# One group of experts fetched by rows from DRAM, and the last pair's output in column ranges

## The chip, the cores and the metric

The kernel runs on one core of a Trainium2 chip. Its time is the device time of one execution in microseconds (us), of which the median over several executions is given. The engines of the core are TensorE (PE, matrix products; PEld is its weight load), VectorE (DVE), ScalarE (ACT), GpSimd (POOL) and SyncE (SP). SP does no arithmetic here: it issues nearly all transfers. A name with q behind it (SPq) is an engine's instruction queue. A core has 16 DMA engines, and each transfer of this kernel is spread over them.

## The reference, cut to what matters

One decoder block on 512 tokens of width 1024, all in float32: a mixer (linear attention beside block-sparse attention), an attention into 256 memory tokens, and a layer of 32 experts, each with a residual add, and a last normalisation. The change lies in the expert layer and behind it.

```python
g_prob = softmax(xt @ w_rg + b_rg); p_grp, grp = top_k(g_prob, 1)      # one of 4 groups
top_p, top_i = top_k(softmax(e_in), 2)                                # two of its 8 experts
weights = p_grp * top_p / sum(top_p); expert = grp * 8 + top_i
# for each expert e with its tokens tok and their weights w:
xb = xt[tok]                                                          # rows of h, 1024 wide
yb = (silu(xb @ w_gate[e]) * (xb @ w_up[e])) @ w_down[e] * w[:, None] # inner width 512
out[tok] += yb
# behind all experts
return rmsnorm(x + out, g_final)
```

## The kernel before, in words

The first half of the kernel (mixer, memory attention, router) ends at about 486 us of the profiled execution. Behind it the 32 experts are worked through as 16 pairs (0 to 15), each expert with 64 slots for tokens; a token's code is its expert and its slot. What doesn't fit 64 slots is done in a loop (`overflow`) that runs as often as the router's result asks; it stands in pair 15, after its second step.

**Gather.** Two pairs, four experts, share one gather of 256 slots: `group_hots` (VectorE) makes 0/1 matrices `oh` (token by slot), and `gather` multiplies them on TensorE with the normalised rows. These are held as two tiles per 128 tokens, `xrh` and `xrl` (a rounded part and the rest, which together give the row). One of its eight steps gives 128 of the 1024 features for 256 slots: 8 products into `g_ps`, then a copy by ScalarE into `xT`, with the gain `gfeat`. The steps are laid between other work of the odd pair and of the even pair behind it. Pairs 0 and 1 have their own gather inside the router's code; seven gathers stand in the loop over the pairs, for pairs 2 and 3 (here called group 1), 4 and 5, and so on.

**One pair.** Eight steps `gate_up` (each two k-rows of gate and up weights for two experts, into `gu_ps`), `hidden` (Silu on ScalarE, a product on VectorE), four transposes `hidden_t`, four steps `down` into `y_ps`, a split into a rounded part and a rest (`rows_hilo`: yh on ScalarE, yl on VectorE), and `combine`: products of yh and yl with the 0/1 rows `ot` into `c_ps`, which VectorE adds into `x`. The `combine` of a pair stands among the steps of the next.

**Weights.** Each pair takes 24 loads of 512 KB (16 of gate and up, 8 of down), 384 in all; below they are numbered 1 to 384 in the order of issue. SP issues them in program order (`load_gate_up`, L938; `load_down`, L944). `eload(n)` lets them be written up to number n at a place of the program: about 33 ahead of the pair at work. Every load takes a block of the pool `bp` (48 blocks of 4 KB per partition); blocks are given out in program order, also to other tiles (`oh`, `xT`, `gf`), and a load waits until the former user of its block is done, and until the load eight before it on SP's queue has landed. `SPILL = 15, 2, 372` says where the loop stands and that loads up to 372 are written ahead of it; the other twelve stand behind it, and every engine passes through the loop's branch (L1267).

**The end.** In the last pair the left 512 columns of `y_ps` are made first, then the right ones; each half is multiplied, added into `x`, squared and summed (`sqj`), the left half is multiplied by the last gain on POOL (`xg`), and `finish` scales and stores: right halves from VectorE through SP's queue (L1389), left halves from ScalarE through its own (L1391).

The order on each engine is that in which the program writes the instructions down; nothing reorders them.

## Time and profile before

| what | value |
|---|---|
| median of 3 executions | 971.14 us (970.98 to 971.64) |
| the profiled execution | 969.94 us |
| its span, first to last instruction | 968.1 us |
| granted TensorE clock, mean | 0.997 |
| PE / DVE / ACT / POOL busy | 949.3 / 471.4 / 312.2 / 32.6 us |
| moved by DMA | 252.47 MB, 250.55 MB of it through one queue |
| DMA share of the span, by queue | 70.2% + 0.3% + 0.3% + 0.3% |

All times in the profile are of one execution. A group row names line, engine, operation and tiles; behind the bar stand its busy time and the mean duration in ns. A row of the chain of waits has a start, a length and what the time went to: an instruction of an engine, or a transfer for which it waited. A row of the windows has the busy time of each engine in that stretch with the number of instructions, the granted clock, and the share and rate of the DMA engines.

### The profile page before, as it was taken

The page shows a single profiled execution, that of the slowest core. Times are in us where ns is not written, and L with a number is a line of the kernel's source. Part 1 is how long each engine was busy: PE and PEld are TensorE (multiplying, and loading weights), DVE is VectorE, ACT ScalarE, POOL GpSimd, SP SyncE. Part 2 cuts the span into 40 slices and gives each one's busy share as a digit, 9 for nine tenths or more (in the row PEclk, how much of TensorE's full clock was granted, in tenths as well). Part 3 has the DMA queues.
Part 4 walks back from the last instruction along what each step waited for, and adds up shares of the span by engine and source line. Part 5 has one row for each costly group of instructions (what it writes and reads, how often), then busy time and mean ns, then how long its engine had stood idle before and what let it go on. Part 6 is the DMA issues. An engine that isn't in the chain of part 4 may idle for free.

```text
span 968.1 us, 13248 instructions
## 1 busy us (share of the span) xinstructions
PE 949.3 (98%) x4969; PEld 619.2 (64%) x4969; DVE 471.4 (49%) x1047; ACT 312.2 (32%) x639; POOL 32.6 (3%) x46
## 2 busy tenths in 40 slices
PE   9999999999999999999999999999999999999995
PEld 7888888878878888888835445454454543545432
DVE  5344872554557846466733254341544414344234
ACT  6452643545565424455321102111021110201103
POOL 3200010000000000000000000000000000000003
PEclk9999999999999999999999999999999999999998
DMA  9512347223253605482689999999999999999983
GB/s 296 171 44 64 68 68 194 65 66 88 66 196 131 196 1 153 124 336 92 260 339 409 408 409 409 409 409 410 408 410 409 409 408 408 409 408 409 409 317 147
DMA packets 114086, 252.47 MB, mean 261 GB/s; under 512 B 10310, under 2 KB 55651, under 8 KB 114020
## 3 DMA queue, kind: packets, MB, share of 16 engines
q1 hardware_dynamic: 113444, 250.55, 70.2%
q10 hardware_dynamic: 576, 1.05, 0.3%
q8 instruction: 40, 0.66, 0.3%
q14 instruction: 26, 0.21, 0.1%
HBM read 247.90 MB, written 3.67 MB: 260 GB/s over the span
## 4 chain that ended last, share of the span: by engine, by line
PE 92%; DVE 3%; ACT 3%; DMA 1%; issue 1%; ACTq 0%; SPq 0%; DVEq 0%
PE gu_ps L136 22%; PE y_ps L136 12%; PE fo L131 8%; PE fo L133 7%; PE fo L132 7%; PE g_ps L136 7%; PE c_ps L136 6%; PE ro L133 3%; PE ro L131 3%; PE ro L132 3%; PE x2o L136 2%; PE xo L132 1%; PE xo L133 1%; PE xo L131 1%; PE mo_ps L136 1%; PE s_ps L136 1%
## 5 line engine op out<-in xcount | busy, mean ns | idle before, releaser
L136 PE MATMUL gu_ps<-we,xT 128*64 128x512 f32 x1024 | 229.0, 595 | 0.4 <-ACT xT L1045 0.3
L136 PEld LDWEIGHTS gu_ps<-we,xT 128*64 128x64 f32 x1024 | 71.0, 137 | 134.0 <-issue 121.5
L206 DVE TENSOR_TENSOR wlo<-wraw,whi 128x1024 fp32r<-128x1024 f32 (+1 forms) x71 | 86.2, 1231 | 77.2 <-ACT whi L205 76.9
L136 PE MATMUL y_ps<-we,hid_t 128*64 128x512 f32 x512 | 114.2, 596 | 0.7 <-ACT hid_t L1238 0.7
L1230 DVE SCALAR_TENSOR_TENSOR hid<-hid,ws,gu_ps 128x512 f32<-128x512 f32 x16 | 12.0, 747 | 171.2 <-PE gu_ps L136 171.2
L131 PE MATMUL fo<-hTh,whi 128*128 128x512 f32 x224 | 89.1, 398 | 0.0
L132 PE MATMUL fo<-hTl,whi 128*128 128x512 f32 x224 | 87.5, 390 | 0.0
L133 PE MATMUL fo<-hTh,wlo 128*128 128x512 f32 x224 | 87.4, 390 | 0.0
L1263 DVE TENSOR_TENSOR x<-c_ps,x 128x512 f32<-128x512 f32 x120 | 75.0, 683 | 20.7 <-PE c_ps L136 20.7
L136 PEld LDWEIGHTS y_ps<-we,hid_t 128*64 128x64 f32 x512 | 35.9, 137 | 69.8 <-issue 60.0
L205 ACT ACTIVATE whi<-wraw 128x1024 fp32r<-128x1024 f32 (+2 forms) x73 | 74.8, 1045 | 4.2 <-DMA wraw<-in_w_in_dram 4.1
L136 PE MATMUL g_ps<-oh,xrh 128*128 128x256 f32 x256 | 66.0, 299 | 1.4 <-DVE oh L1028 1.4
L136 PEld LDWEIGHTS g_ps<-oh,xrh 128*128 128x128 f32 x256 | 47.0, 189 | 30.7 <-issue 24.3
L136 PE MATMUL g_ps<-oh,xrl 128*128 128x256 f32 x256 | 61.6, 281 | 0.0
L1229 ACT ACTIVATE hid<-gu_ps 128x512 f32<-128x512 f32 x16 | 9.6, 597 | 156.8 <-PE gu_ps L136 156.8
L205 ACT ACTIVATE yh<-y_ps 128x512 fp32r<-128x512 f32 x32 | 19.1, 598 | 115.1 <-PE y_ps L136 115.1
L1203 ACT ACTIVATE xT<-g_ps,gfeat 128x256 f32<-128x256 f32 x56 | 25.8, 474 | 89.2 <-PE g_ps L136 57.6
L136 PE MATMUL c_ps<-yh,ot 128*128 128x512 f32 x128 | 52.0, 406 | 0.7 <-ACT yh L205 0.7
L136 PE MATMUL c_ps<-yl,ot 128*128 128x512 f32 x128 | 50.6, 395 | 0.2 <-DVE yl L206 0.2
L131 PEld LDWEIGHTS fo<-hTh,whi 128*128 128x128 f32 x224 | 42.1, 188 | 10.1 <-issue 1.9
L133 PEld LDWEIGHTS fo<-hTh,wlo 128*128 128x128 f32 x224 | 42.0, 188 | 9.1
L136 PEld LDWEIGHTS g_ps<-oh,xrl 128*128 128x128 f32 x256 | 47.1, 189 | 0.6
(321 smaller groups left out, 1487.4 us busy)
## 6 DMA issues: line engine op xcount, KB each, us to landing
we<-in_w_exp_gate_dram SPq DMA_DIRECT2D x128, 512.0 KB, 10.2
we<-in_w_exp_up_dram SPq DMA_DIRECT2D x128, 512.0 KB, 10.2
we<-in_w_exp_down_dram SPq DMA_DIRECT2D x128, 512.0 KB, 10.2
wraw<-in_w_in_dram SPq DMA_DIRECT2D x38, 512.0 KB, 4.1
wraw<-in_w_out_dram SPq DMA_DIRECT2D x8, 512.0 KB, 5.5
wraw<-in_w_ckv_dram SPq DMA_DIRECT2D x8, 512.0 KB, 4.8
wraw<-in_w_proj_gla_dram SPq DMA_DIRECT2D x4, 512.0 KB, 4.3
wraw<-in_w_proj_moba_dram SPq DMA_DIRECT2D x4, 512.0 KB, 4.4
```

The costliest lines, as they stand in the source:

```text
L131: PE.matmul(o, lh, rh, start=first, stop=False)
L132: PE.matmul(o, lh, rl, start=False, stop=False)
L133: PE.matmul(o, ll, rh, start=False, stop=last)
L136: PE.matmul(o, l, r, start=first, stop=last, **kw)
L205: S.activation(hi, src, AF.Copy)
L206: eng.tensor_tensor(lo, src, f(hi), op=ALU.subtract)
L1203: S.activation(xT[k], o, AF.Copy, scale=gfeat[:, k:k + 1])
L1229: S.activation(row, gu[0][0:n], AF.Silu)
L1230: V.scalar_tensor_tensor(row, row, ws[:, 0:1], gu[1][0:n], op0=ALU.mult, op1=ALU.mult)
L1263: V.tensor_tensor(xs, o, xs, op=ALU.add)
```

## The change

Four things are changed.

1. **Group 1 is fetched.** At the end of the router POOL adds `xrh` and `xrl` to four tiles `xp` (blocks of the pool, taken ahead of the loads that are written after them), and stores them through its own queue as a table `xd` of 512 rows in DRAM. It also loads a row of token numbers, `tok`. In pairs 0 and 1, at step k = 5, `fetch` finds on VectorE the token of each of the 128 slots of pairs 2 and 3, and POOL issues an indirect transfer that takes the 128 rows from `xd` into a tile `rows`. `turn` then transposes it in eight squares on TensorE, and ScalarE copies them with the gain into `xT`. `group_hots` and `gather` of group 1 are gone. (The router's token for an empty slot is 0; its weight is 0.)
2. **The loop's limit** goes from 372 to 376 loads.
3. **The last pair's down weights** come as column halves: two blocks of 512 columns and 256 rows, per expert and half, instead of four blocks of whole rows.
4. **The last pair's output** is made in three column ranges, 0 to 511, 512 to 767 and 768 to 1023. The scaled row is written in place into `xo`; three tiles of 128 tokens are stored as whole rows through SP, the last one as two halves.

```diff
-    early = np.concatenate([tri, upper, onehot], axis=1)
+    tokens = np.tile(np.arange(T, dtype=np.float32), (P, 1))
+    early = np.concatenate([tri, upper, onehot, tokens], axis=1)
...
-    SY.dma_start(early, c_early)
+    SY.dma_start(early, c_early[:, 0:512])
...
+    def load_down_halves(e):
+
+        for c in range(2):
+            for q in range(2):
+                b = blk("we", [2, 512])
+                rows = w_exp_down[0][e][2 * q * P:(2 * q + 2) * P, 512 * c:512 * c + 512]
+                SY.dma_start(b, rows.rearrange("(k p) n -> p k n", p=P))
+                yield b
...
-            for loads, n in ((load_gate_up, 2), (load_down, 1)):
+            for loads, n in ((load_gate_up, 2), (load_down_halves if p == NE // 2 - 1 else load_down, 1)):
...
+    xd = dp.tile([T, D], F32, name="xd")
+    for t in range(NT):
+        xp = blk("xp", [D])
+        G.tensor_tensor(xp, f(xrh[t]), f(xrl[t]), op=ALU.add)
+        G.dma_start(xd[tcol(t), :], xp)
+    tok = med("tok", [T])
+    G.dma_start(tok, c_early[:, 512:])
...
+    def fetch(codes):
+
+        oa, ws, idx = med("oa", [T]), small("ws", [2]), small("idx", [1], I32)
+        for i in range(2):
+            V.scalar_tensor_tensor(oa, cw[0][:, i, :], codes, tok, op0=ALU.is_equal, op1=ALU.mult,
+                                   accum_out=ws[:, i:i + 1])
+        V.tensor_tensor(idx, ws[:, 0:1], ws[:, 1:2], op=ALU.add)
+        b = blk("rows", [D])
+        G.indirect_dma_start(b, None, xd[:, :], bass.IndirectOffsetOnAxis(ap=idx[:, 0:1], axis=0))
+        return b
+
+    def turn(rows, xT):
+
+        b = blk("xT", [KD, P])
+        xT.extend(b[:, k, :] for k in range(KD))
+        for k in range(0, KD, 2):
+            t_ps = ps("xt_ps", [2, P])
+            for j in range(2):
+                PE.transpose(t_ps[:, j, :], rows[:, tcol(k + j)], ident)
+            for j in range(2):
+                S.activation(xT[k + j], t_ps[:, j, :], AF.Copy, scale=gfeat[:, k + j:k + j + 1])
+            yield
...
-        s0 = (p % 2) * P
+        s0 = 0 if p // 2 in FETCH else (p % 2) * P
...
-            if p % 2 and p + 1 < NP and k == OH_AT:
+            if (p + 2) // 2 in FETCH and k == 5:
+                fetched[p + 2] = fetch(sid[:, 2 * p + 4:2 * p + 5])
+            if p % 2 and p + 1 < NP and k == OH_AT and (p + 1) // 2 not in FETCH:
                 oh_next = group_hots((p + 1) // 2)
-        if p % 2 and p + 1 < NP:
+        if (p + 1) // 2 in FETCH:
+            xT = []
+            gat = turn(fetched.pop(p + 1), xT)
+        elif p % 2 and p + 1 < NP:
             xT = []
             gat = gather(oh_next, xT, 4 * CAP)
...
-        gs = 1 if p % 2 and p + 1 < NP else 0
+        gs = 1 if (p % 2 or p // 2 in FETCH) and p + 1 < NP else 0
...
-    def last_products(c):
-
-        y = rows_hilo(y_ps[c])
-        yield
-        o = [ps("c_ps", [512]) for t in range(NT)]
+    ranges = (0, 512), (512, 256), (768, 256)
+    ssq, xo = [small("ss4", [4]) for t in range(NT)], [blk("xo", [D]) for t in range(NT)]
+    r = [small("rr", [1]) for t in range(NT)]
+    for t in range(NT):
+        V.memset(ssq[t][:, 3:4], EPS)
+    y_ps.append(ps("y_ps", [256]))
+
+    def x_part(i, t):
...
+    def y_part(i):
+        return y_ps[i][:, 0:ranges[i][1]]
+
+    def last_down(i, fts):
+        a, n = ranges[i]
+        c, a = divmod(a, 512)
+        for ft in fts:
+            for e, (b, own) in enumerate(zip(w, halves)):
+                mm(y_ps[i][own, 0:n], hid_t[:, ft, 64 * e:64 * e + 64], b[8 + 2 * c + ft // 2][:, ft % 2, a:a + n],
+                   ft == 0, ft == 3, skip_group_check=True)
...
+    y = [[med(q, [n], F32R) for q in ("yh", "yl")] for _, n in ranges]
+
+    def high(i):
+        S.activation(y[i][0], y_part(i), AF.Copy)
+
+    def low(i):
+        V.tensor_tensor(y[i][1], y_part(i), f(y[i][0]), op=ALU.subtract)
+
+    def products(i):
+        n = ranges[i][1]
+        o = [ps("c_ps", [512 // n, n]) for _ in range(NT * n // 512)]
...
         for t in range(NT):
-            product(o[t], ot, t, y)
-        yield
-        for t in range(NT):
-            xs = x_half(t, c)
-            V.tensor_tensor(xs, o[t], xs, op=ALU.add)
-            if c == 0 and t == NT - 1:
-                yield
-            S.activation(blk("sqj", [512]), xs, AF.Square, scale=1.0 / math.sqrt(D), accum_out=ssq[t][:, c:c + 1])
-            if c == 0:
-                xg[t] = blk("xg", [512])
-                G.tensor_tensor(xg[t], xs, gf[:, 0:512], op=ALU.mult)
+            product(o[t], ot, t, y[i])
+        return o
+
+    def add(o, i, t):
+        V.tensor_tensor(x_part(i, t), o[t], x_part(i, t), op=ALU.add)
+
+    def square(i, t):
+        S.activation(blk("sqj", [512])[:, 0:ranges[i][1]], x_part(i, t), AF.Square, scale=1.0 / math.sqrt(D),
+                     accum_out=ssq[t][:, i:i + 1])
+
+    def gains(t):
+        G.tensor_tensor(xo[t][:, 0:512], x_part(0, t), gf[:, 0:512], op=ALU.mult)
...
     def scale(t):
         ms = small("ms", [1])
-        V.scalar_tensor_tensor(ms, ssq[t][:, 0:1], EPS, ssq[t][:, 1:2], op0=ALU.add, op1=ALU.add)
...
-        G.tensor_tensor(r, ms, neghalf[:, 0:1], op=ALU.pow)
-        return r
-
-    def finish(t, r):
-        o = blk("xo", [512])
-        V.scalar_tensor_tensor(o, x_half(t, 1), r, gf[:, 512:1024], op0=ALU.mult, op1=ALU.mult)
-        SY.dma_start(out[tcol(t), 512:1024], o)
-        S.activation(xg[t], xg[t], AF.Copy, scale=r)
-        S.dma_start(out[tcol(t), 0:512], xg[t])
-
...
-    for t in range(NT + 1):
-        if t < NT:
-            r[t] = scale(t)
-        if t:
-            finish(t - 1, r[t - 1])
+        V.tensor_reduce(ms, ssq[t], axis=AX.X, op=ALU.add)
+        G.tensor_tensor(r[t], ms, neghalf[:, 0:1], op=ALU.pow)
+
+    def low_half(t):
+        S.activation(xo[t][:, 0:512], xo[t][:, 0:512], AF.Copy, scale=r[t])
+
+    def high_half(t):
+        V.scalar_tensor_tensor(xo[t][:, 512:], x_sb[t][:, 512:], r[t], gf[:, 512:], op0=ALU.mult, op1=ALU.mult)
+
+    last_down(0, range(4))
+    high(0)
+    low(0)
+    last_down(1, range(4))
+    high(1)
+    low(1)
+    last_down(2, range(2))
...
+    last_down(2, range(2, 4))
+    for t in range(NT):
+        add(o0, 0, t)
+        square(0, t)
+        gains(t)
+    for t in range(NT):
+        add(o1, 1, t)
+        if t == 1:
+            high(2)
+        square(1, t)
+        if t == 2:
+            low(2)
+    o2 = products(2)
+    for t in range(NT):
+        add(o2, 2, t)
+        square(2, t)
+        if t >= 2:
+            scale(t - 2)
+    for t in range(NT):
+        if t == 0:
+            scale(2)
+        low_half(t)
+        high_half(t)
+        if t == 0:
+            scale(3)
+        if t + 1 < NT:
+            SY.dma_start(out[tcol(t), :], xo[t])
+    S.dma_start(out[tcol(t), 0:512], xo[t][:, 0:512])
+    SY.dma_start(out[tcol(t), 512:], xo[t][:, 512:])
...
-SPILL = 15, 2, 372
+FETCH = (1,)
+SPILL = 15, 2, 376
```

PE at the end of pair 1's `gate_up` (`xT_3826` is the right half of the first gather's result; the numbers behind `xrh` and `xrl` count tiles of 128 tokens), before:

```order
L136 MATMUL gu_ps<-we,xT_3826 64x512 x16
L136 MATMUL g_ps<-oh,xrh_3812 128x256
L136 MATMUL g_ps<-oh,xrl_3816 128x256
L136 MATMUL g_ps<-oh,xrh_3813 128x256
L136 MATMUL g_ps<-oh,xrl_3817 128x256
L136 MATMUL g_ps<-oh,xrh_3814 128x256
L136 MATMUL g_ps<-oh,xrl_3818 128x256
L136 MATMUL g_ps<-oh,xrh_3815 128x256
L136 MATMUL g_ps<-oh,xrl_3819 128x256
L136 MATMUL c_ps<-yh,ot 128x512
L136 MATMUL c_ps<-yl,ot 128x512
```

and with the change:

```order
L137 MATMUL gu_ps<-we,xT_3826 64x512 x16
L1243 MATMUL xt_ps<-keep,rows 128x128 x2
L137 MATMUL c_ps<-yh,ot 128x512
L137 MATMUL c_ps<-yl,ot 128x512
L137 MATMUL c_ps<-yh,ot 128x512
L137 MATMUL c_ps<-yl,ot 128x512
L1278 MATMUL ht_ps<-keep,hid 128x128 x4
L1243 MATMUL xt_ps<-keep,rows 128x128 x2
```

Eight products of one gather step have become two transposes, which read the fetched tile `rows`; three more such places follow in pair 1, and four in pair 2 for pair 3.

POOL at the start of the experts, with the change (`rr` is the last of the router's normalisations; before, the read of the loop's count, L1306 there, stood right behind it):

```order
L918 TENSOR_TENSOR rr<-ms,neghalf 128x1 x4
L1161 TENSOR_TENSOR xp<-xrh_3812,xrl_3816 128x1024
L1162 DMA xd<-xp 128x1024
L1161 TENSOR_TENSOR xp<-xrh_3813,xrl_3817 128x1024
L1162 DMA xd<-xp 128x1024
L1161 TENSOR_TENSOR xp<-xrh_3814,xrl_3818 128x1024
L1162 DMA xd<-xp 128x1024
L1161 TENSOR_TENSOR xp<-xrh_3815,xrl_3819 128x1024
L1162 DMA xd<-xp 128x1024
L1164 DMA tok<-in_c_early_dram 128x512
L1233 DMA rows<-xd,idx 128x1024 x2
L1348 TENSOR_LOAD rt_xi
```

Ten instructions have come in, seven of them transfers, in this order on one queue.

SP's loads 35 to 40 with the change, with what each waits for (a name with DMAHW is a landing of one of SP's own transfers, DMASW one of POOL's, PE and Pool are the engines that used the block before):

```order
L939 DMA we_4737<-in_w_exp_gate_dram 128x1024 [waits DMAHW7_49,DMASW0_49,Pool_49]
L939 DMA we_4749<-in_w_exp_up_dram 128x1024 [waits DMAHW0_49,PE_49]
L939 DMA we_4751<-in_w_exp_gate_dram 128x1024 [waits DMAHW1_49,PE_49]
L939 DMA we_4753<-in_w_exp_up_dram 128x1024 [waits DMAHW2_49,DMASW1_49,Pool_49]
L939 DMA we_4755<-in_w_exp_gate_dram 128x1024 [waits DMAHW3_49,PE_49]
L939 DMA we_4771<-in_w_exp_up_dram 128x1024 [waits DMAHW4_49,DMASW2_49,Pool_49]
```

Before, each of these waited for its DMAHW and for PE alone. Now loads 35, 38 and 40 (and 45) wait for the landing of a copy into `xd`, whose tile `xp` had the block.

More of the change, by code (lines that the diff above doesn't have):

```diff
@@ L1299, in block_kernel @@
     slot, spill = None, spill_list()
-    comb, gat = iter(()), iter(())
+    comb, gat, fetched = iter(()), iter(()), {}
     for p in range(NP):
@@ L1353, in block_kernel @@
         comb = combine(ot, ys)
-    ssq, xg, r = [small("ss2", [2]) for t in range(NT)], {}, {}
-    def x_half(t, c):
-        return x_sb[t][:, 512 * c:512 * c + 512]
-    def last_products(c):
-        y = rows_hilo(y_ps[c])
-        yield
-        o = [ps("c_ps", [512]) for t in range(NT)]
-        for t in range(NT):
-            product(o[t], ot, t, y)
-        yield
-        for t in range(NT):
-            xs = x_half(t, c)
-            V.tensor_tensor(xs, o[t], xs, op=ALU.add)
-            if c == 0 and t == NT - 1:
-                yield
-            S.activation(blk("sqj", [512]), xs, AF.Square, scale=1.0 / math.sqrt(D), accum_out=ssq[t][:, c:c + 1])
-            if c == 0:
-                xg[t] = blk("xg", [512])
-                G.tensor_tensor(xg[t], xs, gf[:, 0:512], op=ALU.mult)
+    ranges = (0, 512), (512, 256), (768, 256)
@@ new lines, in block_kernel @@
+    y = [[med(q, [n], F32R) for q in ("yh", "yl")] for _, n in ranges]
[6 more added lines that the diff above has]
+        o = [ps("c_ps", [512 // n, n]) for _ in range(NT * n // 512)]
+        o = [b[:, q, :] for b in o for q in range(512 // n)]
+        for t in range(NT):
+            product(o[t], ot, t, y[i])
+        return o
@@ L1382, in scale @@
-        r = small("rr", [1])
-        G.tensor_tensor(r, ms, neghalf[:, 0:1], op=ALU.pow)
-        return r
-    def finish(t, r):
-        o = blk("xo", [512])
-        V.scalar_tensor_tensor(o, x_half(t, 1), r, gf[:, 512:1024], op0=ALU.mult, op1=ALU.mult)
-        SY.dma_start(out[tcol(t), 512:1024], o)
-        S.activation(xg[t], xg[t], AF.Copy, scale=r)
-        S.dma_start(out[tcol(t), 0:512], xg[t])
-    part = [last_products(c) for c in range(2)]
-    for ft in range(4):
-        down(y_ps, hid_t, ft, w, (0,))
@@ L1396, in block_kernel @@
-    next(part[0])
-    for ft in range(2):
-        down(y_ps, hid_t, ft, w, (1,))
-    next(part[0])
-    for ft in range(2, 4):
-        down(y_ps, hid_t, ft, w, (1,))
-    next(part[0])
-    next(part[1])
-    drain(part[0])
-    drain(part[1])
-    for t in range(NT + 1):
-        if t < NT:
-            r[t] = scale(t)
-        if t:
-            finish(t - 1, r[t - 1])
+        V.tensor_reduce(ms, ssq[t], axis=AX.X, op=ALU.add)
+        G.tensor_tensor(r[t], ms, neghalf[:, 0:1], op=ALU.pow)
@@ new lines, in low_half @@
+    def low_half(t):
[9 more added lines that the diff above has]
+    last_down(2, range(2))
+    o0 = products(0)
+    o1 = products(1)
+    last_down(2, range(2, 4))
[3 more added lines that the diff above has]
+        gains(t)
```

2 lines of the change are left out of this document (added).

## Prediction

> **What bounds the kernel now.** I read the page first, then the busy time by stretch, SP's waits, and the chain of waits at the end. The page seems to settle it:
>
> ```profile
> span 968.1 us, 13248 instructions
> PE 949.3 (98%) x4969; PEld 619.2 (64%) x4969; DVE 471.4 (49%) x1047; ACT 312.2 (32%) x639; POOL 32.6 (3%) x46
> ```
>
> TensorE is busy for 98% of the span, so taking matmuls away looks like a gain of their full time. The stretches (columns: PE, PEld, DVE, ACT, POOL busy, PE clock, DMA share, GB/s) say something else about the expert half:
>
> ```profile
> core 0: us, PE busy (x) PEld busy (x) DVE busy (x) ACT busy (x) POOL busy (x), PEclk, DMA share, GB/s
> 474.00:484.00 10.00, 8.35 (x75) 7.84 (x75) 8.27 (x40) 3.00 (x5) 0.56 (x1) 1.00 0.92 371
> 484.00:488.00 4.00, 3.65 (x26) 2.38 (x25) 2.54 (x12) 3.38 (x9) 0.00 (x0) 1.00 0.25 58
> 488.00:500.00 12.00, 12.00 (x60) 4.23 (x58) 3.21 (x8) 2.04 (x4) 0.00 (x0) 1.00 1.00 382
> 500.00:515.00 15.00, 13.38 (x64) 4.50 (x62) 5.39 (x12) 2.39 (x4) 0.00 (x0) 1.00 1.02 409
> 515.00:918.00 403.00, 403.00 (x2026) 190.56 (x2022) 160.60 (x329) 58.10 (x110) 0.00 (x0) 1.00 1.03 409
> ```
>
> From 488 to 918 us the DMA engines have no free time: 409 GB/s at a share of 1.03, for 403 us on end. PE and DMA are both full there; which one is the limit is told by who waits for whom. SP issues the weights, and its waits in 515 to 925 us are:
>
> ```profile
> SPq L938 <- DMA we<-in_w_exp_down_dram: 91.0, 103, 1.6
> SPq L944 <- DMA we<-in_w_exp_up_dram: 46.5, 52, 1.4
> SPq L938 <- PE gu_ps L136: 9.1, 27, 1.0
> ```
>
> SP waits for earlier loads to land, hardly ever for a block that PE must free. So the transfers run as fast as they can, and everything added to them delays each later weight. Last, the end of the chain, and SP's rows around it:
>
> ```profile
> 918.30 7.02 PE y_ps L136 x32
> 925.32 3.46 PE gu_ps L136 x16
> 929.93 7.41 DMA we<-in_w_exp_up_dram
> 937.38 2.79 PE gu_ps L136 x10
> 944.50 5.87 PE y_ps L136 x24
> ```
> ```profile
> we<-in_w_exp_up_dram SPq DMA_DIRECT2D x128, 512.0 KB, 10.2
> ```
> ```profile
> 904.60 0.33 SPq L938 DMA_DIRECT2D we<-in_w_exp_up_dram  x1
> 905.88 0.33 SPq L938 DMA_DIRECT2D we<-in_w_exp_gate_dram  x1
> 907.16 0.33 SPq L938 DMA_DIRECT2D we<-in_w_exp_up_dram  x1
> 918.12 0.33 SPq L938 DMA_DIRECT2D we<-in_w_exp_up_dram  x1
> 928.32 0.33 SPq L938 DMA_DIRECT2D we<-in_w_exp_gate_dram  x1
> 929.93 0.38 SPq L938 DMA_DIRECT2D we<-in_w_exp_up_dram  x1
> ```
> ```profile
> SPq L1267 <- PEq L1267: 7.5, 2, 7.3
> ```
>
> A load is issued every 1.28 us and lands 10.2 us later (eight in flight). Load 372, the last allowed ahead of the overflow loop, is issued at 918.12 and lands about 928.3; SP stands at the loop until PE gets there, and issues the next at 928.32. The load PE needs, number 376, lands at 929.93 + 7.41 = 937.3; PE waits 7.4 us. This is the one place where PE waits for weights.
>
> **The change part by part.**
>
> The gather of group 1 goes. Its eight steps stand in the chain, four of each length (first of each, and the last):
>
> ```profile
> 524.81 1.15 PE g_ps L136 x8
> 527.32 0.96 PE g_ps L136 x8
> 549.01 1.15 PE g_ps L136 x8
> ```
> ```profile
> 365.67 1.04 PE L335 MATMUL tps<-keep,xr 128*128 128x128 f32 x8
> ```
>
> 4 x 1.15 + 4 x 0.96 = 8.4 us leave PE; the 16 transposes that come cost 16 x 1.04 / 8 = 2.1 us. PE gains **6.3 us** by pair 4. Does it reach the end? The first four loads of the last pair end with the one issued at 907.16, landing 917.4; PE takes them up at 925.32, so weights are 7.9 us early. If nothing else changed, PE would still be behind them by 1.6 us in that pair, and would then stand at the loads behind them. This gain is worth something only while DMA is not later. It costs the end nothing either way: I count **0**.
>
> The transfers that come, all through POOL's queue: four copies of 512 KB, the token row of 256 KB, two fetches of 512 KB, 3.41 MB. At 409 GB/s that is **8.3 us** of all engines. What can hide it is idle DMA time. By the shares above (1.03 is full) 1.1 us is free in 474 to 484, 3.0 in 484 to 488, 0.5 up to 515: 4.6 us, and none after. POOL starts the copies here:
>
> ```profile
> 475.60 0.56 POOL L917 TENSOR_TENSOR rr<-ms,neghalf 128x1 f32<-128x1 f32 x1 [8.03 <-DVE ms L915]
> 951.90 5.01 POOL L1377 TENSOR_TENSOR xg<-x,gf 128x512 f32<-128x512 f32 x4 [475.74 <-DVE x L1371]
> ```
>
> after 476.2, with an add of 128x1024 each, twice 5.01 / 4 = 2.5 us, plus an issue by POOL that the trace does not price (I take 1 us, an estimate between SP's 0.33 and the add's 2.5): copies move from about 480, 483, 487 and 490 on, so about two fall into the hole. The fetches (from about 500 and 521) fall outside it.
>
> The blocks that the copies hold. The four xp tiles stand in the program ahead of the 17th load, and there SP was waiting for blocks, not for DMA (its waits in 440 to 490, and issues of loads 25, 32 and 33):
>
> ```profile
> SPq L944 <- PE rk_ps L136: 13.9, 2, 7.0
> SPq L944 <- PE co_ps L136: 11.9, 1, 11.9
> SPq L944 <- PE l_ps L136: 9.5, 3, 3.7
> ```
> ```profile
> 469.54 0.33 SPq L938 DMA_DIRECT2D we<-in_w_exp_gate_dram  x1
> 477.42 0.33 SPq L938 DMA_DIRECT2D we<-in_w_exp_up_dram  x1
> 485.98 0.33 SPq L938 DMA_DIRECT2D we<-in_w_exp_gate_dram  x1
> ```
>
> So each load from the 17th gets the block that the fourth after it had: load 28 goes at 477.42, and loads 29 to 32, before issued by then, wait for 485.98 and later. Four loads, 4 x 1.28 = **5.1 us** of transfer, move out of a time with free DMA into the full one. Together: 8.3 + 5.1, less at most 4.6 of idle time, is 8.8. Bounds: with no loss by the blocks and all idle time used 8.3 - 4.6 = 3.7; with none used 13.4. I take **+9**: the sum with the hole nearly filled, since two copies and the delayed loads meet it.
>
> [...]
>
> The loop's limit moves from 372 to 376 loads. Without the stop load 376 would land at 928.3 + 4 x 1.28 = 933.4, not 937.3. With the change the weights are late, PE reaches the loop about when load 364 has landed, and SP gets there with eight loads (10.2 us) in flight; its own stop would have to last that long to leave a hole. **-3.9 us**; bounds -3.9 and, if SP's stop drains the queue again, 0.
>
> The last pair. Down loads in halves: columns 0 to 511 are whole four loads before the end, and the rest is needed 3.5 us later; PE's 7.1 us from 937.38 to 944.50 cover the first. If the 2 KB pieces run at 380 instead of 409 GB/s, 0.8 us over eight loads. 0. Behind the products, the last chain:
>
> ```profile
> 960.23 3.11 SPq L1389 DMA_DIRECT2D out_dram<-xo  x4
> 963.69 0.34 ACTq L1391 DMA_DIRECT2D out_dram<-xg  x1
> ```
> ```profile
> GB/s 0 0 0 0 0 0 0 0 0 0 0 290 387 380 402 365 365 395 365 395 372 373 402 357 410 358 380 402 365 387 365 112 0 0 0 0 0 0 0 0
> DMA packets 1152, 2.10 MB, mean 191 GB/s; under 512 B 128, under 2 KB 128, under 8 KB 1152
> ```
>
> (958 to 969 us.) Once the first rows go out at 960.2, 2.10 MB take 5.6 us at about 380 GB/s without a break: the bytes set the end, not the order of the arithmetic. The last range has 256 columns instead of 512, which shortens its adds and squares by some 2 us, but the middle range's four adds and four squares now stand ahead of them on the same two engines. I count the first store as early as before, whole rows of 4 KB at 409 GB/s (5.1 us): **-0.4**; bounds -2 and +1. Memsets, the 14 DVE operations of fetch against 9 of the one-hots, and the copies of the turned tiles lie on engines with waits of their own: 0, or under 1 us if PE had no DMA to wait for.
>
> Sum: -3.9 + 9 - 0.4 = **+4.7 us**. Against the profiled execution's own 969.94 us (1.8 over its span) that is 974.6; the runs shown have their median at 971.14, so **975.8**. From the bounds of the transfers alone, 3.7 and 13.4: 970.5 to 980.2.
>
> **The rivals.**
>
> *Absorbed* (faster). The copies and fetches cost the weights 0 to 2 us: POOL's queue fills the hole, the blocks come back in time, and two queues together move more than one. Then only the closed stop counts: 971.1 - 3.9 - 0.4 = 966.8, to 968.8. For it: 4.6 us of idle time, and a PE wait of 7.4 us that the table's 376 goes straight at. Against it: after 488 us no idle time is left for the fetches, 2.6 us by themselves, and the output rows, with two queues at work, show 380 GB/s, not more than 409.
>
> *Balanced* (no change). Half of the delayed loads are made up: the transfers cost 4 to 5 us, as much as the stop gave: 970.5 to 972. For it: the lower bound is 3.7.
>
> *PE first*. If DMA were not the limit, the 6.3 us would arrive: 971.1 - 6.3 - 0.4 and a PE wait gone: below 964. SP's waits for DMA, 103 times in the first row alone, speak against it.
>
> *Copies hold the queue* (much slower). Loads 35, 38, 40 and 45 wait in SP's order for the blocks of the four copies. If POOL takes 10 us for each add and issue instead of 3.5, the last copy lands about 516, SP stands still with eight loads in flight from about 505, and DMA idles some 6 us more: 982. It decides from the fourth copy landing after about 506.
>
> *It doesn't do what it says*: if the fetched rows land after 525, PE waits for them in place of the gather. The fetch can go at about 500; even behind eight loads it lands by 512. Little chance, and at the end hidden by the same DMA limit.
>
> **How the numbers follow.** My forecast (transfers +6 to +13) 0.62; copies hold the queue 0.06; balanced 0.14; absorbed 0.14; PE first 0.04. Runs of before differ by 0.7 us, and 0.2% (1.9 us) is about what can be told from no change. Slower 0.68, same 0.14, faster 0.18. Own range of the forecast 972.5 to 980; the range given reaches to the absorbed case: 967.5 to 980.5.
>
> **What would show it.** Right: DMA at 409 GB/s from about 484 with POOL's queue beside SP's; the last loads landing 5 us later than before; DMA waits of PE from about pair 9 on, 6.3 + 9 - 7.9 = 7.4 us of them in all, in place of the one 7.4 us wait at the loop, and SP issuing load 377 with the queue still full; group 1 shorter on PE by 6 us; outputs within 1 us of before, counted from the last pair's first product. Wrong: load 60 landing less than 4 us later than before (then the transfers were hidden), PE without waits to the end, or a hole in DMA after 500 (then the copies hold the queue).

## The result: 984.6 us, 1.4% slower

The change takes 984.59 us (median of 4 runs, 984.06 to 985.44); the kernel before, beside it, 971.39. The ratio is 1.0137, with a 95% interval of 1.0125 to 1.0150: 13.2 us slower. The forecast was 975.8, range 967.5 to 980.5. The direction was right, the size was not: the measured time lies above the range.

The page of the changed kernel starts:

```profile
span 982.6 us, 13252 instructions
PE 950.5 (97%) x4945; PEld 620.3 (63%) x4945; DVE 478.2 (49%) x1057; ACT 313.8 (32%) x656; POOL 47.5 (5%) x57
```

TensorE's busy time is as before (949.3), though group 1's products are gone: the gate and up products take 234.7 us in place of 229.0. POOL has eleven instructions more (57 for 46), four adds and seven transfers. The same stretches as in the prediction (PE, PEld, DVE, ACT, POOL busy, PE clock, DMA share, GB/s), of the change:

```profile
474.00:484.00 10.00, 7.78 (x71) 7.38 (x70) 9.62 (x24) 3.04 (x5) 7.06 (x6) 1.00 1.01 401
484.00:488.00 4.00, 0.18 (x1) 0.00 (x0) 3.48 (x11) 0.00 (x0) 2.55 (x2) 0.74 0.75 306
488.00:500.00 12.00, 10.59 (x54) 6.58 (x54) 6.20 (x21) 4.34 (x10) 3.49 (x3) 0.80 0.51 181
500.00:515.00 15.00, 13.37 (x65) 4.70 (x66) 6.84 (x18) 2.34 (x4) 1.13 (x1) 1.00 1.02 410
```

From 474 to 484 VectorE is busy for 9.62 us with 24 instructions (before: 8.27 with 40). From 484 to 488 TensorE has next to nothing to do, and from 488 to 500 its granted clock is 0.80 (before: 1.00) and DMA, full before, is half idle. From 500 on everything looks as before, only later. Where the time comes in is told by the start of each pair's gate and up products (first row of `gu_ps` of each pair in the timeline):

| | before | change | later by |
|---|---|---|---|
| pair 0 | 486.30 | 494.10 | 7.80 |
| pair 2 | 541.05 | 545.01 | 3.96 |
| pair 4 | 600.32 | 601.61 | 1.29 |
| pair 8 | 718.64 | 720.98 | 2.34 |
| pair 12 | 836.96 | 845.22 | 8.26 |
| pair 15 | 925.15 | 935.59 | 10.44 |
| end of pair 15's gate and up | 940.17 | 954.84 | 14.67 |
| end of the span | 968.1 | 982.6 | 14.5 |

(0.65 of each difference is there at the first expert load, 409.51 against 410.16, 67 us ahead of POOL's first add.) Four things stand in this table: pair 0 starts late; group 1 gives back 6.5 us by pair 4, as predicted; TensorE loses 9.2 us on the way from pair 4 to pair 15, waiting for weights (the gate and up products of pairs 7, 9, 11 and 13 take 15.0 to 17.1 us, before 13.9); and pair 15 itself takes 4.2 us longer. Behind it nothing changes: the end is as long as before, within 0.2.

**Why pair 0 is late.** POOL's queue at the end of the router (start, duration), with the four adds and the first and last copy:

```profile
476.79 2.38 POOL L1161 TENSOR_TENSOR xp<-xrh,xrl 128x1024 f32<-128x1024 f32 x1
479.49 0.80 POOL L1162 DMA_DIRECT2D xd<-xp  x1 [0.32 <-POOL xp L1161]
480.31 2.41 POOL L1161 TENSOR_TENSOR xp<-xrh,xrl 128x1024 f32<-128x1024 f32 x1
...
483.63 2.35 POOL L1161 TENSOR_TENSOR xp<-xrh,xrl 128x1024 f32<-128x1024 f32 x1
...
490.73 2.34 POOL L1161 TENSOR_TENSOR xp<-xrh,xrl 128x1024 f32<-128x1024 f32 x1 [3.88 <-DVE route L1065]
493.36 0.57 POOL L1162 DMA_DIRECT2D xd<-xp  x1 [0.30 <-POOL xp L1161]
```

and three instructions of VectorE in the router, with the change:

```profile
476.83 2.62 DVE L1038 SCALAR_TENSOR_TENSOR oh<-keep,rt_code,oha 128x256 fp32r<-128x256 int16 x1
...
480.32 2.43 DVE L1012 TENSOR_SCALAR pen<-keep,pos 128x4 f32<-128x4 f32 x1
...
483.73 2.30 DVE L1016 TENSOR_SCALAR route<-keep,pos 128x32 f32<-128x32 f32 x1
```

The same three before:

```profile
476.16 0.48 DVE L1028 SCALAR_TENSOR_TENSOR oh<-keep,rt_code,oha 128x256 fp32r<-128x256 int16 x1
...
478.42 0.23 DVE L1002 TENSOR_SCALAR pen<-keep,pos 128x4 f32<-128x4 f32 x1
...
479.62 0.24 DVE L1006 TENSOR_SCALAR route<-keep,pos 128x32 f32<-128x32 f32 x1
```

An instruction on 4 numbers per partition takes 2.43 us instead of 0.23: 480.32 + 2.43 = 482.75, and POOL's add ends at 480.31 + 2.41 = 482.72. The other two end 0.05 and 0.28 us behind POOL's adds (486.03 and 485.98; 479.45 and 479.17). So VectorE stands while POOL adds (below: the lock), three times, 2.14 + 2.20 + 2.06 = 6.4 us (the fourth add has no instruction of VectorE beside it), and the router's last step waits for VectorE (the ranks of the last tokens, and the first product of pair 0), first with the change, then before:

```profile
487.52 0.18 PE L137 MATMUL rk_ps<-rt_OHb,route 128*128 128x32 bf16 x1 [5.49 <-DVE rt_OHb L1020]
...
494.10 5.37 PE L137 MATMUL gu_ps<-we,xT 128*64 128x512 f32 x24 [0.30 <-ACT xT L1055]
```
```profile
481.36 0.18 PE L136 MATMUL rk_ps<-rt_OHb,route 128*128 128x32 bf16 x1
...
486.30 5.37 PE L136 MATMUL gu_ps<-we,xT 128*64 128x512 f32 x24 [0.35 <-ACT xT L1045]
```

The ranks come 6.2 us later (5.5 without the 0.65). The rest, 1.6 us, is added between the two rows, 6.6 us apart instead of 4.9; there, behind its stand, TensorE was granted a clock of 0.50 (488 to 492).

Not every VectorE instruction stands beside POOL. In the run with the adds alone (below) three adds follow each other without a break, from 476.15 to 483.38, and beside the second of them five instructions of VectorE, from 478.75 to 479.66, take 0.09 to 0.25 us (before: 0.09 to 0.26). Four additions of `c_ps` (PSUM) into `x` at the end of the kernel before take 2.48 us beside POOL's products (from 951.08 on) and 2.48 us nearly without them (from 956.24 on). Of the three instructions that stood, `oh` reads two tensors, the other two one tensor and a column of numbers; what decides which instructions stand isn't shown.

**Why pair 15 is long.** TensorE's gate and up products of pair 15, and SP's issues around the loop, load 376 and load 377, with the change:

```profile
935.59 3.60 PE L137 MATMUL gu_ps<-we,xT 128*64 128x512 f32 x16
942.62 12.22 PE L137 MATMUL gu_ps<-we,xT 128*64 128x512 f32 x48 [3.44 <-DMA we<-in_w_exp_gate_dram]
```
```profile
939.58 0.33 SPq L939 DMA_DIRECT2D we<-in_w_exp_up_dram  x1
942.64 7.99 SPq L954 DMA_DIRECT2D we<-in_w_exp_down_dram  x8
```

TensorE is at the loop at 939.2 and goes on at 942.62, when SP issues again. The row puts the wait down to a transfer. But the next products read loads 365 to 368, and the last of these landed at 939.51, so weights can account for 0.3 of the 3.44 us; the experiments show that it is the loop.

### The profile page after: what moved, and what is told of

It is laid out like the page before. It is cut to its first block, busy times and chain, and to the rows that moved or that the text cites. A ratio compares the mean times of both kernels' runs of the same rounds, so it can differ in the third digit from the quotient of the medians.

```text
span 982.6 us, 13252 instructions
## 1 busy us (share of the span) xinstructions
PE 950.5 (97%) x4945; PEld 620.3 (63%) x4945; DVE 478.2 (49%) x1057; ACT 313.8 (32%) x656; POOL 47.5 (5%) x57
## 3 DMA queue, kind: packets, MB, share of 16 engines
q0 software_dynamic: 944, 3.41, 0.9%
## 4 chain that ended last, share of the span: by engine, by line
PE 80%; DMA 12%; DVE 4%; ACT 2%; issue 1%; POOL 0%; SPq 0%; DVEq 0%; ACTq 0%
PE gu_ps L137 18%; PE y_ps L137 9%; PE fo L132 7%; PE fo L134 7%; PE fo L133 7%; DMA we<-in_w_exp_up_dram 5%; PE g_ps L137 5%; PE c_ps L137 5%; DMA we<-in_w_exp_gate_dram 4%; PE ro L133 3%; PE ro L134 3%; PE ro L132 3%; DMA we<-in_w_exp_down_dram 2%; PE x2o L137 2%; PE xo L133 1%; PE xo L134 1%
## 5 line engine op out<-in xcount | busy, mean ns | idle before, releaser
L137 PE MATMUL gu_ps<-we,xT 128*64 128x512 f32 x1024 | 234.7, 600 | 7.4 <-DMA we<-in_w_exp_gate_dram 6.2
L137 PEld LDWEIGHTS gu_ps<-we,xT 128*64 128x64 f32 x1024 | 73.9, 137 | 146.6 <-issue 119.0
L137 PE MATMUL y_ps<-we,hid_t 128*64 128x512 f32 (+1 forms) x528 | 113.6, 582 | 1.3 <-ACT hid_t L1280 1.0
L137 PEld LDWEIGHTS g_ps<-oh,xrh 128*128 128x128 f32 x224 | 41.7, 194 | 32.0 <-issue 26.6
L137 PE MATMUL g_ps<-oh,xrh 128*128 128x256 f32 x224 | 58.3, 304 | 1.4 <-DVE oh L1038 1.4
L137 PE MATMUL g_ps<-oh,xrl 128*128 128x256 f32 x224 | 53.8, 282 | 0.0
L137 PE MATMUL c_ps<-yh,ot 128*128 128x512 f32 (+1 forms) x132 | 52.9, 403 | 0.7 <-ACT yh L1428 0.7
L137 PE MATMUL c_ps<-yl,ot 128*128 128x512 f32 (+1 forms) x132 | 51.0, 389 | 0.1
L133 PEld LDWEIGHTS fo<-hTl,whi 128*128 128x128 f32 x224 | 42.1, 188 | 8.1
L1222 ACT ACTIVATE xT<-g_ps,gfeat 128x256 f32<-128x256 f32 x48 | 22.2, 474 | 76.6 <-PE g_ps L137 49.5
## 6 DMA issues: line engine op xcount, KB each, us to landing
we<-in_w_exp_gate_dram SPq DMA_DIRECT2D x128, 512.0 KB, 10.2
we<-in_w_exp_up_dram SPq DMA_DIRECT2D x128, 512.0 KB, 10.2
we<-in_w_exp_down_dram SPq DMA_DIRECT2D x128, 512.0 KB, 10.2
```

Of the source, the lines that this page charges most:

```text
L133: PE.matmul(o, lh, rl, start=False, stop=False)
L137: PE.matmul(o, l, r, start=first, stop=last, **kw)
L1222: S.activation(xT[k], o, AF.Copy, scale=gfeat[:, k:k + 1])
```

## The experiments

Each run's time stands beside runs of the kernel before on the same chip; the differences below are against those. Load 84 (a load of pair 3, well inside the full stage) serves as the measure of how late the weights are: it is issued at 546.79 before and at 563.35 in the change, 16.6 later, 15.9 without the 0.65.

```profile
546.79 0.33 SPq L938 DMA_DIRECT2D we<-in_w_exp_up_dram  x1
```
```profile
563.35 0.33 SPq L939 DMA_DIRECT2D we<-in_w_exp_up_dram  x1
```

**No fetch.** The change without its first part: `FETCH = ()`, and these lines out:

```diff
-    xd = dp.tile([T, D], F32, name="xd")
-    for t in range(NT):
-        xp = blk("xp", [D])
-        G.tensor_tensor(xp, f(xrh[t]), f(xrl[t]), op=ALU.add)
-        G.dma_start(xd[tcol(t), :], xp)
-    tok = med("tok", [T])
-    G.dma_start(tok, c_early[:, 512:])
```

> The change without its fetch: group 1 is gathered by products as before, and nothing is stored to or read from the table of rows; the loop's limit of 376, the column halves and the column ranges stay. Theory L (POOL's adds hold VectorE up on the router's path, and nearly all of the loss comes from there): the pairs stand where they stood before; the last pair's gate and up products take 13.9 us instead of 15.0, since no load is missing any more, and the end gives 0.2: 969.9. The prediction's terms taken as they stood (stop -3.9, end -0.4): 966.8. If the loss sits in the new end or in the limit: above 975.

Measured: 968.25 against 971.32, ratio 0.9970 (0.9958 to 0.9981), 3.1 us faster. All of the loss sits in the fetch or comes through it; limit and end together are a gain, larger than theory L had it.

**Adds alone, blocks alone.** On the kernel without the fetch, in the place of the lines above:

```diff
+    for t in range(NT):
+        xp = blk("xp", [D])
+        G.tensor_tensor(xp, f(xrh[t]), f(xrl[t]), op=ALU.add)
```

and, for the blocks, one column written by ScalarE:

```diff
+        S.activation(xp[:, 0:1], f(xrh[t])[:, 0:1], AF.Copy)
```

> As the run without the fetch, but with POOL's four adds of 128x1024 into four blocks at their place; their result is used by nothing, no copy and no fetch follows. Theory L: three VectorE instructions of the router last as long as the add beside them (2.3 to 2.6 us instead of 0.2 to 0.5), pair 0 starts about 7 us later than before, and since TensorE has work without a break up to the last pair, the end comes 7 us later: 977. Rival (it is the 3.41 MB of transfers): as without the fetch, 970, whatever POOL does. Rival (blocks): the loads come 5 us later, the end moves by at most 2 us, pair 0 starts as before.

> As the run without the fetch, but four blocks are taken where the four tiles of the copies stood, each written in one column by ScalarE and then free; no add, no transfer. Theory L: load 17 waits until about 464 instead of 442, loads 29 to 32 about 10 us longer, the weights from load 84 on come about 5 us later than before; pair 0 starts as before; the weights were 7.9 us early at the last pair, so the end stays within 1 us of the run without the fetch: 970 to 971. Rival (the moved blocks are the main loss): 975 or more.

Measured: adds 977.95, ratio 1.0071 (1.0052 to 1.0089); blocks 971.64, ratio 1.0001 (0.9992 to 1.0011). Pair 0 starts at 492.65 with the adds and at 487.16 with the blocks. Load 84, adds first, then blocks, then the kernel without the fetch:

```profile
557.55 0.33 SPq L939 DMA_DIRECT2D we<-in_w_exp_up_dram  x1
```
```profile
552.44 0.33 SPq L939 DMA_DIRECT2D we<-in_w_exp_up_dram  x1
```
```profile
547.01 0.33 SPq L939 DMA_DIRECT2D we<-in_w_exp_up_dram  x1
```

Against 547.01 the blocks make 5.4 (4.7 after the offset of that run's first load, 0.7), and the prediction had 5.1. The adds make 10.5 (10.6 with that run's offset, -0.1): 5.9 more than the blocks that they take as well. No transfer is added in either kernel, so bytes alone don't explain the loss: the adds alone, with their blocks, cost 9.7 us at the end, 6.3 more than the blocks (977.95 and 971.64). The blocks cost more at the end than theory L said (3.4 us over the kernel without the fetch, not 0 to 1); why is seen below.

**The add on ScalarE.** One line of the change:

```diff
-        G.tensor_tensor(xp, f(xrh[t]), f(xrl[t]), op=ALU.add)
+        S.activation(xp, x_sb[t], AF.Copy, scale=r2[t])
```

The copied rows have the columns in x's order here, not in that of `xrh`, so group 1's products work on other features; nothing is left out.

> The change with one instruction replaced: ScalarE writes the row times its scale into the copy's tile (one pass of 128x1024) in place of POOL's add; copies, fetches and blocks stay. Theory L: no VectorE instruction of the router lasts longer than before, pair 0 starts within 1 us of before instead of 7.8 later, load 84 comes about 9 us later instead of 16, and the time is 973 to 977. Rival (transfers and blocks are the loss): load 84 stays 16 us late, 984.

Measured: 983.23, ratio 1.0117 (1.0092 to 1.0141). Pair 0 starts at 487.02, so the lock is gone, but the time is not what theory L gave. One reason is a new wait (the columns: us in total, times, longest):

```profile
PE ht_ps L1278 <- DVE hid L1272: 9.0, 1, 9.0
...
DVE oa L1229 <- DMA tok<-in_c_early_dram: 4.1, 1, 4.1
```

The token row stood behind the four copies in POOL's queue, and VectorE stood at its wait for it with `hidden` of pair 0 behind. So, in the next kernel, the token row goes first, and the copy is written in `xrh`'s order:

```diff
+    tok = med("tok", [T])
+    G.dma_start(tok, c_early[:, 512:])
     for t in range(NT):
         xp = blk("xp", [D])
-        G.tensor_tensor(xp, f(xrh[t]), f(xrl[t]), op=ALU.add)
+        S.activation(xp.rearrange("a (q j p) -> a q j p", p=P, j=2), paired(x_sb[t]), AF.Copy, scale=r2[t])
```

> As the run with ScalarE in place of POOL's add, but the token row is loaded ahead of the four copies (in that run VectorE seems to have stood at its wait for the token row, with hidden of pair 0 behind it, some 8 us), and the copy is written in the column order of xrh. Theory D: the stall of TensorE between pairs 0 and 1 goes, pair 4 starts 3 us earlier than in the change, but load 370 stays about 13.7 us behind the run without the fetch (8.3 by bytes, 5.4 by blocks), and the end stays at 980 to 983. Theory L (without the lock the loss is half): 973 to 977.

Measured: 981.74 against 970.78, ratio 1.0117 (1.0098 to 1.0135), +11.0. The stall shrank from 9.0 to 4.8 us and did not go: ScalarE writes the slots' weights (`wts`) at 502.05, without the fetch at 493.46, and why it does so that late isn't shown. Even so pair 4 starts at 600.78, about as without the fetch (600.45), and the time is 13.5 us above that kernel's: theory L falls, as the account of the whole loss. Load 84 is at 560.26, 13.3 behind the kernel without the fetch (13.1 without that run's offset): 4.7 by blocks, 8.3 by bytes, none of them hidden, since ScalarE writes the copies only from 489.1 on, when the idle time is over. Against the change (+13.2) the lock, less what the later copies cost, is worth 2.2 us at the end.

**The table made from x itself.** `xrh` and `xrl` aren't needed for it: POOL's queue stores `x_sb[t]`, and the fetched rows are normalised by ScalarE at step k = 4 of the pair between fetch and transposes. No add, no block. Early, behind each tile's last sum:

```diff
         c_scale(t)
+        G.dma_start(xd[tcol(t), :], x_sb[t])
...
+    def normalise(rows):
+        ss, ms, rr = small("ss2", [2]), small("ms", [1]), small("rr", [1])
+        for c in range(2):
+            S.activation(med("sqj", [512]), rows[:, 512 * c:512 * c + 512], AF.Square, scale=1.0 / math.sqrt(D),
+                         accum_out=ss[:, c:c + 1])
+        V.scalar_tensor_tensor(ms, ss[:, 0:1], EPS, ss[:, 1:2], op0=ALU.add, op1=ALU.add)
+        G.tensor_tensor(rr, ms, neghalf[:, 0:1], op=ALU.pow)
+        S.activation(rows, rows, AF.Copy, scale=rr)
...
-                PE.transpose(t_ps[:, j, :], rows[:, tcol(k + j)], ident)
+                PE.transpose(t_ps[:, j, :], paired(rows)[:, k // 2, j, :], ident)
```

or late, all five transfers at the place of the change:

```diff
+    tok = med("tok", [T])
+    G.dma_start(tok, c_early[:, 512:])
     for t in range(NT):
-        xp = blk("xp", [D])
-        G.tensor_tensor(xp, f(xrh[t]), f(xrl[t]), op=ALU.add)
-        G.dma_start(xd[tcol(t), :], xp)
+        G.dma_start(xd[tcol(t), :], x_sb[t])
```

> The change, with the table made otherwise: POOL's queue stores each tile of x itself, as soon as it is complete (from about 453 us on, where DMA is less than half busy), with no add and no block; the fetched rows are normalised by ScalarE in the pair between fetch and transposes. Theory D (the stream of weights sets the end; what counts is by how much it is late at about load 370, less some 1.8 us in hand, as the first four runs have it: 5.6 late gave 3.4, 10.8 gave 9.7): only the two fetches and the token row, 1.31 MB, 3.2 us, fall into the full stage; pair 0 starts as before, pair 4 6 us earlier, and the end comes 1 to 2 us behind the run without the fetch: 969.5, 968.5 to 971. Rival P (TensorE sets the end): the 6.3 us of products arrive, 962. Rival Q (POOL's transfers are held up beside VectorE): the copies land 10 us late or more, and the end is above 973.

> The change with the table of x itself (no add, no block), but all five of POOL's transfers at the place of the change, the token row first, so from about 476 us on. Prediction's term (idle time takes up part of the copies): DMA has some 4 us free between 474 and 488, so load 84 comes 4 to 6 us later than without the fetch, and with the loop's cost of some 2.8 us the time is 973 to 975. Rival (idle time hides nothing, as in the run with the token row first, where 8.3 us of bytes and 5 of blocks made 13.3): load 84 8.3 us later, 976 to 978.

Measured: early 971.20 against 970.78, ratio 1.0002 (0.9992 to 1.0011); late 971.79 against 970.90, ratio 1.0007 (0.9998 to 1.0017). Load 84 is issued at 550.02 and 550.40, both about 3 us behind the kernel without the fetch. Late, the copies go out within 2.15 us and fill the gap that was there from 484 to 488 (share 0.25 before):

```profile
477.67 2.15 POOL L1162 DMA_DIRECT2D xd<-x  x4
```
```profile
484.00:488.00 4.00, 3.65 (x29) 2.87 (x30) 2.54 (x12) 2.70 (x8) 0.00 (x0) 1.00 1.01 414
```

The late table's forecasts, 973 to 975 and 976 to 978, were both too high. So idle time does hide the copies where they are issued in time for it: 3.41 MB cost 3 us of lateness, about what the two fetches and the rest behind 488 take. The rival "idle time hides nothing" falls; it was right for a kernel whose copies come at 490 only. Rival P falls as well: TensorE starts pair 4 6.3 us earlier than without the fetch (594.18 against 600.45), and the end is no earlier. Rival Q falls too: the early copies land 5.5 us after their issue (median of four), and the end is below 973. The early table ends 0.2 us above theory D's range, and the row that says why names no transfer (TensorE, early table):

```profile
922.58 3.60 PE L137 MATMUL gu_ps<-we,xT 128*64 128x512 f32 x16
929.53 12.13 PE L137 MATMUL gu_ps<-we,xT 128*64 128x512 f32 x48 [3.35 <-PEq L1316]
```

L1316 is the loop.

**The loop's limit.** Four kernels differ from others in `SPILL[2]` alone: without the fetch 372 instead of 376, and 380; the change with 372; the early table with 372. A fifth is the kernel before with 376.

> The run without the fetch, with the loop's limit back at 372. The gate and up products of the last pair took 15.0 us before and 13.9 with the limit of 376: if that is all that the stop costs, 969.4. By the prediction's term (3.9 us, read from the chain's row of 7.41 us): 972.2.

> The change with the loop's limit back at 372, the fetch as it is. Theory D: the load that TensorE waits for in the last pair (about number 371) lies ahead of the stop, and TensorE passes the loop about when load 372 is issued, so the stop costs nothing: 984 to 986. By the prediction's term: 988.5.

> The early table of x with the loop's limit back at 372. Theory S (new, from the runs with late weights): SP needs about 3.1 us from its last issue ahead of the loop until it issues again behind it (939.58 to 942.64 in the change, 926.48 to 929.55 with the early table), and every engine leaves the loop together; so with a limit of 376 TensorE, which is there at 926.2, stands 3.4 us, and its clock falls behind the stand. With 372 SP is there 5 us earlier, this wait goes, and the time falls from 971.2 to 968 to 969.5. Rival (only the weights' lateness counts): 971.

> The run without the fetch, with the loop's limit at 380 instead of 376. Theory S: load 380 is issued at about 923.1 + 4 x 1.28 = 928.3, SP issues again at 931.3, and TensorE, at the loop at 928.5, stands about 2.9 us: 970.8 to 972. Rival (a later stop is never worse): 968.3 or less.

> The kernel before with nothing changed but the loop's limit, 376. From the runs without the fetch (968.3 with 376, 970.3 with 372): 2.0 us faster, 968.8 to 969.4. By the prediction's term: 3.9 faster, 967.2.

| kernel | limit 372 | limit 376 | limit 380 |
|---|---|---|---|
| before, old end | 0 | -2.5 (0.9972, 0.9962 to 0.9982) | |
| no fetch | -0.5 (0.9996, 0.9986 to 1.0005) | -3.1 (0.9970) | +2.0 (1.0017, 1.0008 to 1.0027) |
| early table | -2.2 (0.9976, 0.9965 to 0.9987) | +0.4 (1.0002) | |
| the change | +11.0 (1.0112, 1.0094 to 1.0130) | +13.2 (1.0137) | |

(us against the kernel before, with ratio and interval.) The limit of 376 is a gain of 2.5 to 2.6 us where the weights are early, and a loss of 2.2 to 2.6 where they are late. The forecast for the change with 372 (984 to 986, or 988.5) missed: it got faster, 981.78. The early table with 372 came as forecast (968.66); without the fetch, 372 gave 970.29, between its two figures, and 380 gave 972.92, 0.9 above its range; the limit alone (968.45) came 0.4 below its range. TensorE and SP there, in the change with 372, at the same place:

```profile
935.41 7.89 PE L137 MATMUL gu_ps<-we,xT 128*64 128x512 f32 x34
943.67 1.08 PE L137 MATMUL gu_ps<-we,xT 128*64 128x512 f32 x4 [0.37 <-DMA we<-in_w_exp_gate_dram]
```
```profile
934.23 0.33 SPq L939 DMA_DIRECT2D we<-in_w_exp_up_dram  x1
938.59 0.33 SPq L939 DMA_DIRECT2D we<-in_w_exp_gate_dram  x1
```

The weights are as late as in the change (load 370 lands at 941.79 against 942.08), and TensorE works straight through the place at 939 where it stood 3.44 us in the change. So that wait was for the loop, not for a transfer. SP needs about 3.1 us from its last issue ahead of the loop to its next behind it, also where it hardly waits for others (939.58 to 942.64; 926.48 to 929.55 with the early table; 0.4 us of waits in each). The instructions of the loop's own line in the change say who came last (number, duration, first and last start):

```profile
L1309 SPq EVENT_SEMAPHORE  x28: 17/17/17, 939.9 to 942.5; - x28
L1309 PEldq EVENT_SEMAPHORE  x8: 51/51/51, 934.8 to 942.5; - x8
L1309 DVEq EVENT_SEMAPHORE  x8: 21/21/21, 936.6 to 942.5; - x8
```

TensorE's queue (PEldq) is there at 934.8, VectorE's at 936.6, SP's at 939.9 (POOL's is first recorded at 940.7); the last row of each is at 942.5. The stand follows from this: SP's last issue plus 3.1 us, less the end of TensorE's sixteen products, is 3.5 us in the change (measured 3.44). With 380, in the kernel without the fetch, this can be made at will: TensorE is at the loop at 929.2 and goes on when SP comes; 928.61 + 3.1 - 929.21 is 2.5 us (measured 2.48).

```profile
925.61 3.60 PE L137 MATMUL gu_ps<-we,xT 128*64 128x512 f32 x16
931.70 10.52 PE L137 MATMUL gu_ps<-we,xT 128*64 128x512 f32 x48 [2.48 <-PEq L1302]
```

With 372 the opposite happens: SP leaves a gap in the transfers (before: load 373 is issued 10.2 us after 372). What TensorE lost by this gap is the difference between two pairs of before:

```profile
865.99 13.90 PE L136 MATMUL gu_ps<-we,xT 128*64 128x512 f32 x64
925.15 15.02 PE L136 MATMUL gu_ps<-we,xT 128*64 128x512 f32 x64
```

1.1 us in the products; the gain by 376 is 2.5 in all. The two profiled executions differ by 1.5 us (spans of 968.1 and 966.6); the rest stands in executions without a trace. The last products behind a stand are also slow in some kernels: 48 of them take 12.22 us in the change, and 10.52 in the kernel with 380. The granted clock says so: in the change 0.83 from 940 to 950. What decides when the clock falls isn't settled here; a stand of 2.15 us (blocks alone) was followed by 0.59 for 4 us, one of 2.48 (380) by 1.00 from 928 to 948. It may differ between executions of one kernel: with 380 three of ten took 971.1 to 971.8 us (mean clock 0.995 to 0.996; the trace is of one of these) and seven 972.7 to 973.7 (0.994 to 0.995); with blocks alone five took 970.6 to 970.9 and five 972.4 to 973.1 (the trace is of one of these), so the blocks' 3.4 us is the middle of 2.4 and 4.3.

With this the blocks are understood too: in that run load 376 is late (928.71), and TensorE stands at the loop:

```profile
926.01 3.60 PE L137 MATMUL gu_ps<-we,xT 128*64 128x512 f32 x16
931.76 12.22 PE L137 MATMUL gu_ps<-we,xT 128*64 128x512 f32 x48 [2.15 <-DMA we<-in_w_exp_gate_dram]
```

Three kernels are faster than the one before, and cannot be told apart: no fetch 968.25, the limit alone 968.45, the early table with 372 968.66. Only the last has the fetch: its 6.3 us of TensorE bring nothing that shows at the end.

## Why the prediction was wrong

The three terms of the sum, each measured by runs that differ in it alone:

| term | predicted | measured | from |
|---|---|---|---|
| loop's limit | -3.9 | +2.2 | the change with 376 and with 372: 13.2 - 11.0 |
| transfers of the fetch | +9 | +11.5 | with 372, with and without the fetch: 11.0 + 0.5 |
| the end | -0.4 | -0.5 | no fetch, 372 |
| sum | +4.7 | +13.2 | |

**The loop's limit** is the step that failed, by 6.1 of the 8.5 us. It failed twice. First in the reading: "PE waits 7.4 us" was taken from a row of the chain of waits, "929.93 7.41 DMA". That row is the time of a transfer on the chain, from SP's issue to the landing; TensorE was at work meanwhile. The timeline row of the same products, 15.02 us against 13.90 of another pair, is not in the prediction: 1.1 us lost, not 7.4. So -3.9 was a bound of the transfers, not of TensorE; in the kernel before it is worth -2.5. Second, the loop was seen as SP's stop only. Its other side, that TensorE waits there for SP, stood in two rows that the prediction quotes: SP issues at 918.12 and next at 928.32, 10.2 us, and waits 7.3 of them. (The row says for TensorE's queue; by the loop's line VectorE's came later.)

```profile
L1267 PEldq EVENT_SEMAPHORE  x8: 51/51/51, 924.3 to 928.2; - x8
L1267 DVEq EVENT_SEMAPHORE  x8: 21/21/21, 926.2 to 928.2; - x8
```

The other 2.9 are SP's way through, and they are harmless only as long as SP comes early. The prediction asked what a late SP does to the queue ("would have to last that long to leave a hole") and not who else stands there. What it said of the queue held: DMA's share is 1.03 from 936 to 950. The bounds, "-3.9 and 0", didn't hold the sign.

The split depends on the order. Without the fetch the limit is worth -2.6, and the fetch then costs 16.3 (13.2 + 3.1). The 4.8 us between the two ways belong to neither term alone: the fetch makes the weights late, and late weights turn the limit's gain into a loss. The prediction priced the limit with late weights, so the table's way is the one to hold against it.

**The transfers.** Of the parts of +9, the bytes (8.3) and the blocks (5.1, measured 4.7) were right in size. What was missed is a part that has no byte in it: POOL's add. The prediction took its duration for POOL (2.5 us, measured 2.4), placed the copies by it, and showed VectorE's 8.27 of 10 us just there (474 to 484) in its rows, without asking what an add on POOL does to VectorE. The runs put it at 5.9 us of lateness of the weights and 6.2 us of pair 0. Its price was to be had from before. VectorE's scaling of the first rows, three times, by duration (least, median, most, in ns), then a subtraction on POOL and the slowest of the three beside it:

```profile
L307 DVE SCALAR_TENSOR_TENSOR xr<-xi,rr,gmix x3: 1287/1287/1996, 12.7 to 21.2; 128x1024 f32<-128x1024 f32 x3
```
```profile
12.22 1.37 POOL L206 TENSOR_TENSOR wlo<-wraw,whi 128x544 fp32r<-128x544 f32 x1 [1.12 <-ACT whi L205]
```
```profile
12.68 2.00 DVE L307 SCALAR_TENSOR_TENSOR xr<-xi,rr,gmix 128x1024 f32<-128x1024 f32 x1
```

0.7 us more than its like, while POOL's subtraction, which began ahead of it, ends at 13.6. The remaining 5.3 of the 15.9 us are, as far as the parts add up, the bytes less 3.0 that the gap hid; the prediction let the gap hide 4.6. Its sum for the weights, 8.8, was thus short by the 5.9 of the adds and 1.6 of the gap, less 0.4 of the blocks. At the end, 15.9 us of late weights are 11.5 of time, with 372: some of them had been in hand.

**The end** was right (-0.5 for -0.4), and so was the gain that counts for nothing: TensorE gains 6.5 us by pair 4 and has lost them between pairs 8 and 12 (later by 2.34, then 8.26). The waits for weights came from pair 7 on, 9.2 us up to pair 15 (the prediction: from about 9 on, 7.4).

**The rivals.** "Copies hold the queue" gave 982, near the result, and a gap in DMA; the gap came (half of 488 to 500), but the fourth copy landed at 497.45, not behind 506, and SP stood there for blocks that the late router still used. Its waits from 440 to 560 with the change:

```profile
SPq L945 <- PE rk_ps L137: 34.5, 1, 34.5
...
SPq L939 <- DVE oh L1038: 10.6, 1, 10.6
```

The first is load 17, moved by the four blocks; the second is load 29, which waits for VectorE's 0/1 rows (before: 5.1 us). That POOL's transfers might be held up beside VectorE (rival Q) isn't borne out: in the late table POOL issues five transfers from 476.87 to 479.82 beside a VectorE that is busy for 8.27 of 10 us, 0.80 us for the first and 2.15 for the other four, and the weights are 3 us late. "PE first" falls with the early table: 6.3 us at pair 4, nothing at the end. "Absorbed" is what a kernel without the add and the blocks does, up to the fetches.

## What to carry to other kernels

Work that is given to an idle engine can have a price on its neighbour (here 6.4 us of VectorE for three adds of 2.4): before an add goes to POOL, look for VectorE instructions beside POOL's in the same trace, and compare them with their like. At a point that all engines pass, ask of each how long it needs to get there and through, not only who is waited for now; a limit that is right while one engine is early (2.5 us gained in the kernel before) is wrong when it is late (2.2 us lost in the change). And a row of the chain is the time of what it names, not idle time of the engine behind it: the engine's own row tells that.

## What the runs showed of the hardware

- A POOL addition of two 128x1024 tiles (2.35 to 2.41 us) held up three VectorE instructions of 0.23 to 0.48 us until it ended (they took 2.30 to 2.62 us), down to one on 4 numbers per partition. Instructions between the adds, on tiles as small, took their usual time (0.09 to 0.25 us), and so did five beside an add in the run with the adds alone; four additions with a PSUM input took 2.48 us beside POOL's products and nearly without them.
- SP's way through the loop took 3.1 us from the last issue ahead of it to the first behind it, with 0.4 us of waits for others. It runs 28 semaphore instructions there, TensorE's queue 8; why SP has more isn't shown.
- Copies of 512 KB through POOL's queue took 0.53 to 0.80 us to issue, and the last one of the change landed after 4.1 us (493.36 to 497.45, DMA share 0.73); the indirect fetches took 1.0 to 1.6 us to issue, and in the change 8.9 and 8.3 us to land in the full stage (DMA share 1.03).
- A wait of TensorE was put down to a transfer in the change and in the run with the blocks, and to the loop (PEq) in those with the early table and with 380, at the same instruction.
